# Attention scores as whole-array matmuls of stacked, rounded operands that GpSimd prepares, in a two-layer encoder

## The chip, the cores and the metric

The kernel runs on one core of one Trainium2 chip. A core has a matrix engine (TensorE, in the profile PE, and PEld for its loads of weights), VectorE (DVE), ScalarE (ACT), GpSimd (POOL) and a queue engine (SP) that issues transfers. The metric is the device time of one execution in microseconds.

## The reference, cut to what matters

Two layers on 256 tokens of 1024 numbers, in float32. Layer 0 mixes tokens by a gated convolution, layer 1 by attention in a window; behind each stands a retrieval of experts by product keys (PEER). The change touches the scores of the attention:

```
qkv = x @ w_qkv                       # 16 query heads, 4 key/value heads, 64 numbers each
scores = einsum("bnqhgd,bnkhd->bnhgqk", q, kw) / sqrt(HEAD_DIM)
logits = where(valid, scores + bias, NEG_INF)
probs  = softmax(concat([logits, sink_logit]))[..., :-1]
out    = einsum("bnhgqk,bnkhd->bnqhgd", probs, vw) @ w_o
```

With 256 tokens and a window of 128 a head has a score matrix of 256 x 256, cut to the window by its bias.

## The kernel before, in words

Nearly all products are made on TensorE in a rounded float32 form (F32R) that TensorE takes faster than full float32. To keep the precision each weight tile is split: ScalarE rounds it (`hi`, L189) and VectorE takes the remainder (`lo`, L190). The activations are kept as such pairs too, and a product is the sum of lo x hi, hi x hi and hi x lo. The weights stream through SP's queue in one fixed order; `take` hands out the next pair and starts the split of a later one.

The attention (`attention`) comes between the two PEER parts and lasts from about 874 to 960 us in the profile. It starts with the keys (`bk`), query block 0 and the values. A query block is 128 columns, two heads of 64, one on partitions 0 to 63 and one on 64 to 127, and there are eight blocks. `factors` and L455 scale the keys, L756 makes the factor of the queries, L758 scales query block 0 and L674 the others. Queries and keys lie in full float32 in `qk`. Key block n holds the two key heads that query blocks 4n to 4n + 3 use.

Then a loop of eleven steps: step s does `values(s-3)` (tile po), `scores(s)` (psc), `turned(s-2)` (transposes of the probabilities, ppt), `project(s-4)` (pwo), `queries(s+2)` (pq) and `softened(s)` (the softmax, on ScalarE and VectorE), as far as these exist. `in_turn` puts each behind TensorE's last instruction, so that TensorE runs them in this order; the other engines' instructions are placed by a scheduler that goes by readiness. `scores(c)` before: for each half of the tokens t and each of the two heads i a matmul of 64 partitions in full float32, which the profile shows as two instructions:

```
r = slice(HD * i, HD * i + HD)
matmul(b[i][:, t], qk[r, c, P * t : P * t + P], qk[r, kc], start=True, stop=True)
```

VectorE adds bias to the scores and takes the row minimum (L690) straight from PSUM.

GpSimd's queue holds only transfers here: in steps 0, 2, 4, 6 and 8 `blank_part` (L570) writes zeros over a part of the table that the second PEER part will fill. Each part waits for the transfer of the one before and for the last remainder that VectorE has made (`bg.behind`).

Of the kernel before, what the change touches and what calls it, by code (L numbers as in the profile page):

```python
# [8 lines left out]
F32 = mybir.dt.float32  # L9
F32R = mybir.dt.float32r  # L10
# [4 lines left out]
ALU = mybir.AluOpType  # L15
AX = mybir.AxisListType

P = 128
T = 256
D = 1024  # L20
NT = T // P
KC = D // P
HEADS = 16
HD = 64
# [52 lines left out]
def trunk_kernel(  # L77
# [21 lines left out]
    V, S, G, PE = nc.vector, nc.scalar, nc.gpsimd, nc.tensor  # L99

    const = ctx.enter_context(tc.tile_pool(name="const", bufs=1))
    big = ctx.enter_context(tc.tile_pool(name="big", bufs=1))
# [8 lines left out]
    def matmul(*a, **k):  # L111
        newest[:] = [PE.matmul(*a, **k).ins]  # L112
        return newest[0]
# [5 lines left out]
    def in_turn():  # L119

        return tc.issue_after(newest[0])
# [11 lines left out]
    def bank(tag, name):  # L133
        if tag == "acc":
            return four_banks(False).tile([P, 512], F32, tag=tag, name=name, bufs=4)
        return ps.tile([P, 512], F32, tag=tag, name=name, bufs=2)
# [77 lines left out]
    def take(n=2):  # L214

        prefetch(n)
        return ahead.popleft()
# [8 lines left out]
    def cols_product(dst, w, act, nth=None):  # L226

        hi, lo = (a.rearrange("p (k c) -> p k c", k=KC) for a in w)
        if nth == 0:
            turns = [(w, k, n) for w, n in ((hi, 0), (lo, 0), (hi, 1)) for k in range(KC)]  # L230
        elif nth == 1:
            turns = [(w, k, n) for w, n in ((hi, 0), (hi, 1), (lo, 0)) for k in range(KC)]
        else:
            turns = [(lo, k, 0) for k in range(KC)] + [(hi, k, n) for k in range(KC) for n in range(2)]
        for i, (w, k, n) in enumerate(turns):
            matmul(dst, w[:, k], act[:, k, T * n : T * n + T], start=(i == 0), stop=(i == 3 * KC - 1))
# [216 lines left out]
    def times_factor(dst, b, n):  # L453

        V.tensor_tensor(  # L455
            dst, b.rearrange("p (a t) -> p a t", a=n), yb[:, None, :].to_broadcast([P, n, T]), ALU.mult
        )
# [190 lines left out]

    def attention(sc, last):
        bias, sk = sc.held  # L650
        qk = sc(10, T)
        vt = sc(NT, T)
        both = big.tile([P, 2, KC, 2 * T], F32R, tag="HB", name="xo")
        bk = bank("u", "pk")
# [2 lines left out]

        ring = [(sc(2, 2, T + 1), sc(2, 2, 2, P), sc(2, 2, 2)) for i in range(3)]
        yq = sc(T)

        def all_values(i, bv):
            hi, lo = (a.rearrange("p (k c) -> p k c", k=4) for a in take())
            for t in range(NT):
                for k in range(4):
                    xh = xn[:, 4 * i + k, P * t : P * t + P]
                    xl = xn[:, 4 * i + k, T + P * t : T + P * t + P]
                    matmul(bv[t][:, :T], xh, lo[:, k], start=(i == 0 and k == 0), stop=False)
                    matmul(bv[t][:, :T], xh, hi[:, k], start=False, stop=False)
                    matmul(bv[t][:, :T], xl, hi[:, k], start=False, stop=(i == 1 and k == 3))

        def queries(c):
            b = bank("acc" if 4 <= c < 6 else "g", "pq")
            cols_product(b[:, :T], take(), xn)
            V.tensor_tensor(qk[:, c], b[:, :T], yq, ALU.mult)  # L674

        def scores(c):

            p, _, s = ring[c % 3]
            kc = KC + c // 4
            V.tensor_copy(p[:, :, :, T], sk[:, 2 * c : 2 * c + 2, None].to_broadcast([P, 2, NT]))  # L680
            b = [bank("u", "psc").rearrange("p (t k) -> p t k", t=2) for i in range(2)]
            for t in range(NT):
                for i in range(2):
                    r = slice(HD * i, HD * i + HD)
                    matmul(b[i][:, t], qk[r, c, P * t : P * t + P], qk[r, kc], start=True, stop=True)
            for t in range(NT):
                for i in range(2):
                    j0 = 383 - P * (1 - t)
                    h = 2 * c + i
                    V.tensor_tensor_reduce(  # L690
                        p[:, i, t, :T], b[i][:, t], bias[:, h, j0 : (j0 - T if j0 >= T else None) : -1],
                        1.0, sk[:, h : h + 1], ALU.add, ALU.min, s[:, 0, i, t : t + 1],
                    )
# [48 lines left out]
        def do(f, c, *a):  # L742
            with in_turn():
                f(c, *a)

        cols_product(bk[:, T:], take(), xn, 1)
        b0 = bank("u", "pq")
# [6 lines left out]
        with tc.issue_after(evicted[0]):  # L754
            copied[:] = [S.activation(stat[:, 10:11], eps, AF.Exp).ins]
        V.tensor_scalar(yq, yb, -1.0 / 8.0, None, op0=ALU.mult)  # L756
        times_factor(qk[:, KC:], bk, 2)
        V.tensor_tensor(qk[:, 0], b0[:, :T], yq, ALU.mult)  # L758
        with in_turn():
            all_values(1, pair)  # L760
        do(queries, 1)
        for t in range(NT):
            S.activation(vt[:, t], pair[t][:, :T], AF.Copy, scale=stat[:, 8 + t : 9 + t])

        for s in range(KC + 3):
            if s in (0, 2, 4, 6, 8):
                blank_part(nc.gpsimd, bg.behind)
            if s >= 3:
                do(values, s - 3)
            if s < KC:  # L770
                do(scores, s)
            if s == KC - 1:
                do(project, s - 4, lambda: do(turned, s - 2))
            else:
                if 2 <= s < KC + 2:
                    do(turned, s - 2)
                if 4 <= s < KC + 2:
                    do(project, s - 4)
            if s + 2 < KC:
                do(queries, s + 2)  # L780
            if s < KC:
                with tc.issue_after(copied[0]):
                    softened(s)
# [498 lines left out]
    sc = Scratch("HA", "mix0")  # L1282
# [11 lines left out]
    last = peer(0, last, prepare_attention)  # L1294
    blank_table()
    last = attention(held.pop(), last)

    def last_row(part):
# [49 lines left out]
    for n, (t, c) in enumerate(ends):  # L1348
        h = c.start // 512
        if c.start == 768:  # L1350
            b = bank("u", "pend")[:, :T]
# [99 lines left out]
```

## Time and profile before

| | us |
|---|---|
| median of 3 runs | 1740.62 (1739.82 to 1740.95) |
| profiled execution | 1739.6 |
| its span | 1737.8 |
| TensorE busy | 1729.0 |
| VectorE busy | 1383.1 |
| GpSimd busy | 995.4 |
| in the stretch 866 to 960: TensorE, VectorE, ScalarE, GpSimd busy, of 94.0 | 93.9, 68.9, 64.3, 5.8 |

A row of the profile names line, engine, operation, the tile written and the tile read. The chain goes back from the last instruction to whatever released each step. In the groups, busy time counts overlapping instructions once, while the mean duration of a matmul holds its way through the array as well. The granted clock of TensorE is 0.999 of full speed over the span.

### The profile page before, as it was taken

How to read it: one execution, taken by the hardware profiler on the slowest of the kernel's cores; microseconds unless marked ns; L12 is line 12 of the kernel's file. 1: busy time of each engine (PE TensorE's matmuls, PEld its weight loads, DVE VectorE, ACT ScalarE, POOL GpSimd, SP SyncE). 2: the span in 40 equal slices, each digit the busy share in tenths (PEclk: the TensorE clock that was granted, in tenths of full speed). 3: DMA queues.
4: the chain of work that ended last, by engine and by line, in shares of the span. 5: the costliest groups of instructions: out<-in, count | busy, mean ns of one | idle time of the engine just before them, and what ended most of it. 6: DMA issues, size and time to landing. Idle time of an engine off the chain costs nothing.

```text
span 1737.8 us, 28407 instructions
## 1 busy us (share of the span) xinstructions
PE 1729.0 (99%) x9801; PEld 1486.7 (86%) x9801; DVE 1383.1 (80%) x2996; ACT 946.9 (54%) x1274; POOL 995.4 (57%) x592
## 2 busy tenths in 40 slices
PE   9999999999999999999999999999999999999998
PEld 8989888888898888888898898888888888888886
DVE  8879999887877677777686899898887867777776
ACT  5455665565555444444476656655655544444444
POOL 1002888878888888500000048888788888881000
PEclk9999999999999999999999999999999999999999
DMA  7786998777769899998765779987776799997884
GB/s 246 245 285 212 277 280 197 169 190 171 183 182 237 226 238 242 286 286 260 228 207 169 255 212 284 256 196 171 190 176 164 202 240 230 236 246 251 259 261 148
DMA packets 292592, 390.80 MB, mean 225 GB/s; under 512 B 120181, under 2 KB 209813, under 8 KB 292192
## 3 DMA queue, kind: packets, MB, share of 16 engines
q1 hardware_dynamic: 86976, 314.35, 54.1%
q0 software_dynamic: 79904, 22.17, 14.4%
q10 hardware_dynamic: 125568, 52.48, 11.6%
q8 instruction: 76, 1.25, 0.3%
q14 instruction: 68, 0.56, 0.1%
HBM read 352.95 MB, written 35.95 MB: 224 GB/s over the span
## 4 chain that ended last, share of the span: by engine, by line
PE 98%; DVE 1%; DMA 1%; issue 0%; ACT 0%; SPq 0%; ACTq 0%
PE ph L112 41%; PE pv L112 40%; PE pq L112 6%; PE pconv L112 3%; PE pgate L112 1%; PE psc L112 1%; PE pwo L112 1%; PE pout L112 1%; PE pg L112 1%; PE ppt L116 0%; PE po L112 0%; PE pk L112 0%; DVE xs L335 0%; DMA gates<-table 0%; DMA xs<-in_x 0%; PE ptr L116 0%
## 5 line engine op out<-in xcount | busy, mean ns | idle before, releaser
L190 DVE TENSOR_TENSOR lo<-raw,hi 128x1024 fp32r<-128x1024 f32 (+1 forms) x597 | 722.5, 1220 | 227.4 <-ACT hi L189 163.3
L189 ACT CAST hi<-raw 128x1024 fp32r<-128x1024 f32 x595 | 623.7, 1050 | 489.1 <-PE pv L112 163.1
L582 POOL DMA_INDIRECT table<-route x256 | 448.5, 1752 | 130.0 <-issue 71.9
L112 PE MATMUL pv<-hi,xn 128*128 128x512 f32 (+1 forms) x2048 | 507.9, 389 | 0.0
L112 PE MATMUL ph<-xn,hi 128*128 128x512 f32 (+1 forms) x2112 | 491.4, 385 | 0.0
L112 PEld LDWEIGHTS pv<-hi,xn 128*128 128x128 f32 x2048 | 384.3, 188 | 79.7
L112 PEld LDWEIGHTS ph<-xn,hi 128*128 128x128 f32 x2112 | 380.3, 188 | 70.6
L582 POOL DMA_INDIRECT far_table<-yb x192 | 379.6, 1977 | 58.6 <-issue 51.0
L112 PE MATMUL pv<-lo,xn 128*128 128x512 f32 x1024 | 277.3, 390 | 0.3 <-DVE lo L190 0.2
L112 PEld LDWEIGHTS ph<-xn,lo 128*128 128x128 f32 x2048 | 262.0, 191 | 9.1
L112 PE MATMUL ph<-xn,lo 128*128 128x256 f32 x2048 | 269.2, 284 | 0.0
L112 PEld LDWEIGHTS pv<-lo,xn 128*128 128x128 f32 x1024 | 191.3, 188 | 40.3 <-ACT xn L1243 1.0
L1220 POOL DMA_DIRECT2D far_gates<-far_table x44 | 23.9, 543 | 231.0 <-DVE route L1237 115.4
L570 POOL DMA_DIRECT2D table<-blank x16 | 18.7, 1168 | 214.5 <-DVE lo L190 164.2
L582 POOL DMA_INDIRECT set_table<-yb x64 | 117.3, 1833 | 26.0 <-issue 18.6
L1243 ACT CAST xn<-hm 128x512 fp32r<-128x512 f32 x64 | 39.9, 623 | 76.8 <-PE pv L112 64.8
L1244 DVE TENSOR_TENSOR xn<-hm,xn 128x512 fp32r<-128x512 f32 x64 | 44.1, 690 | 37.6 <-ACT xn L1243 25.2
L295 ACT COPY hm<-ph 128x512 f32<-128x512 f32 x62 | 36.4, 587 | 58.7 <-PE ph L112 31.1
L112 PE MATMUL pq<-xr,hi 128*128 128x512 f32 (+1 forms) x288 | 65.7, 373 | 0.2
L1174 ACT ACTIVATE hm<-hm 128x512 f32<-128x512 f32 x62 | 39.1, 631 | 41.8 <-DVE hm L296 41.6
L112 PEld LDWEIGHTS pq<-xr,hi 128*128 128x128 f32 x288 | 50.4, 188 | 9.8 <-ACT xr L379 0.8
L295 ACT COPY route<-ph 128x512 f32<-128x512 f32 x62 | 36.1, 583 | 28.4 <-PE ph L112 23.6
(218 smaller groups left out, 1518.2 us busy)
## 6 DMA issues: line engine op xcount, KB each, us to landing
raw<-in_u SPq DMA_DIRECT2D x256, 512.0 KB
raw<-in_v SPq DMA_DIRECT2D x256, 512.0 KB
table<-blank POOLq DMA_DIRECT2D x16, 1024.0 KB
raw<-in_w_q SPq DMA_DIRECT2D x32, 512.0 KB
gates<-table ACTq DMA_DIRECT2D x128, 128.0 KB
raw<-in_w_in SPq DMA_DIRECT2D x23, 512.0 KB
far_table<-blank ACTq DMA_DIRECT2D x10, 1024.0 KB
far_gates<-far_table ACTq DMA_DIRECT2D x156, 64.0 KB
```

What stands on the lines that cost most here:

```text
L112: newest[:] = [PE.matmul(*a, **k).ins]
L189: bg.rounded = (G.tensor_copy if pieces > 1 else S.copy)(hi[:, c], raw[:, c]).ins
L190: bg.behind = V.tensor_tensor(lo[:, c], raw[:, c], hi[:, c].bitcast(F32), ALU.subtract).ins
L295: S.copy(dst, b[:, :, T:])
L570: ins = queue.dma_start(dst, blank[:, None, :].to_broadcast([P, dst.shape[1], P])).ins
L582: nc.gpsimd.indirect_dma_start(to, bass.IndirectOffsetOnAxis(ap=places[:, c : c + 1], axis=0), gates[:, c : c + 1], None, compute_op=ALU.a ...
L1174: S.activation(hm[:, j : j + 2], hm[:, j : j + 2], AF.Gelu)
L1220: ins = (nc.gpsimd if i == 2 else nc.scalar).dma_start(f[:, i], part.rearrange("p (a e t) -> p a e t", a=2, e=2)).ins
L1243: copied[:] = [S.copy(a[:, 0], src).ins]
L1244: return V.tensor_tensor(a[:, 1], src, a[:, 0].bitcast(F32), ALU.subtract).ins
```

## The change: what it does, and the diff

The scores are made of rounded operands. For each head a query block is laid out over all 128 partitions: its rounded half on the head's own 64 partitions, its remainder on the other 64 (`stacked_query`). The keys are laid out twice over the 128 partitions: once the rounded keys on both halves, once their remainders on both halves (`stacked_keys`). A matmul with the first sums rounded query x rounded key and remainder x rounded key, one with the second adds the two other products, in the same bank. A call of scores is now eight matmuls of 128 partitions where it was eight instructions of 64.

The copies that round and the subtractions that leave the remainder are new instructions of 64 partitions x 256 numbers. For a query block they are two roundings and two subtractions on GpSimd; block 0 has its subtractions on VectorE. For key block 0 ScalarE rounds the own halves, GpSimd the others, VectorE and GpSimd subtract; for key block 1 GpSimd does all eight. The stacks take the place of a tile of the PEER part before (`xa`), and the scaled queries go to a ring of two.

```
-        qk = sc(10, T)
+        kf, qf = sc(2, T), [sc(T) for _ in range(2)]
...
+        stacks = big.tile([P, KC, 2 * T], F32R, tag="xa", name="stacks").rearrange("p k c -> p (k c)")
+        keys = stacks[:, : 8 * T].rearrange("p (n i s c) -> p n i s c", n=2, i=2, s=2)
+        query = [stacks[:, 2 * T * (4 + i) : 2 * T * (5 + i)].rearrange("p (i c) -> p i c", i=2) for i in range(3)]
+        sides = slice(0, HD), slice(HD, P)
+
+        def stacked_keys(n, rounds, subtracts):
+            for i, (own, other) in enumerate((sides, sides[::-1])):
+                rounds(keys[own, n, i, 0], kf[own, n])
+                G.tensor_copy(keys[other, n, i, 0], kf[own, n])
+                for to, subtract in ((own, subtracts), (other, G.tensor_tensor)):
+                    subtract(keys[to, n, i, 1], kf[own, n], keys[own, n, i, 0].bitcast(F32), ALU.subtract)
+
+        def stacked_query(c, b, subtracts):
+            q, to = qf[c % 2], query[c % 3]
+            V.tensor_tensor(q, b, yq, ALU.mult)
+            for i, (own, other) in enumerate((sides, sides[::-1])):
+                G.tensor_copy(to[own, i], q[own])
+                subtracts(to[other, i], q[own], to[own, i].bitcast(F32), ALU.subtract)
...
-            V.tensor_tensor(qk[:, c], b[:, :T], yq, ALU.mult)
+            stacked_query(c, b[:, :T], G.tensor_tensor)
...
-                    r = slice(HD * i, HD * i + HD)
-                    matmul(b[i][:, t], qk[r, c, P * t : P * t + P], qk[r, kc], start=True, stop=True)
+                    for s in range(2):
+                        matmul(
+                            b[i][:, t], query[c % 3][:, i, P * t : P * t + P], keys[:, c // 4, i, s],
+                            start=(s == 0), stop=(s == 1),
+                        )
...
-        times_factor(qk[:, KC:], bk, 2)
-        V.tensor_tensor(qk[:, 0], b0[:, :T], yq, ALU.mult)
+        times_factor(kf, bk, 2)
+        stacked_query(0, b0[:, :T], V.tensor_tensor)
+        stacked_keys(0, S.copy, V.tensor_tensor)
         with in_turn():
             all_values(1, pair)
         do(queries, 1)
+        stacked_keys(1, G.tensor_copy, G.tensor_tensor)
```

GpSimd's order at the attention, before the change; the first row is the end of the PEER part, `route` with `in_subk` the start of the next one (mix is the scratch of the attention, set_table and far_table are tables of the PEER part):

```order
L582 DMA far_table_110<-yb 1048576x1 x32
L582 DMA far_table_111<-yb 1048576x1 x32
L1220 DMA far_gates<-far_table_111 128x128 x22
L570 DMA table<-blank 128x16x128 x5
L793 DMA route_9840<-in_subk 128x2048
```

The five blanks follow each other with nothing between. After the change, GpSimd's first rows behind far_gates; L667 and L668 are the roundings of the keys on their own and on the other partitions, L670 the keys' remainders, L676 and L677 rounding and remainder of a query block:

```order
L668 CAST stacks<-mix_7407 64x256 x2
L676 CAST stacks<-mix_7407 64x256 x2
L670 TENSOR_TENSOR stacks<-mix_7407,stacks 64x256 x2
L667 CAST stacks<-mix_7407 64x256
L668 CAST stacks<-mix_7407 64x256
L670 TENSOR_TENSOR stacks<-mix_7407,stacks 64x256 x2
L667 CAST stacks<-mix_7407 64x256
L668 CAST stacks<-mix_7407 64x256
L670 TENSOR_TENSOR stacks<-mix_7407,stacks 64x256 x2
L570 DMA table<-blank 128x16x128
L676 CAST stacks<-mix_7407 64x256 x2
L677 TENSOR_TENSOR stacks<-mix_7407,stacks 64x256 x2
```

The first three rows belong to key block 0 and query block 0, the six behind them to key block 1, then come the first blank and query block 1. Behind these stand query block 2, the second blank, query block 3, the third blank, query blocks 4, 5 and 6, the fourth blank, query block 7 and the fifth blank.

VectorE's order at the same place, with its waits, after the change (L455 scales the keys, the first L674 query block 0, the second query block 1; L190 are remainders of weights for the next query products):

```order
L455 TENSOR_TENSOR mix_7407<-pk,yb 128x512
L674 TENSOR_TENSOR mix_7407<-pq,mix_7407 128x256 [waits DVE_49]
L670 TENSOR_TENSOR stacks<-mix_7407,stacks 64x256 [waits Activation_49] x2
L677 TENSOR_TENSOR stacks<-mix_7407,stacks 64x256 [waits Pool_49] x2
L190 TENSOR_TENSOR lo<-raw,hi 128x1024 [waits DMAHW3_49,PE_49]
L190 TENSOR_TENSOR lo<-raw,hi 128x1024 [waits DMAHW4_49,PE_49,Activation_49]
L674 TENSOR_TENSOR mix_7407<-pq,mix_7407 128x256 [waits PE_49]
```

Before the change the rows L670 and L677 were not there and the first L674 was L758; now the four subtractions stand ahead of the two L190, and the second pair of them waits for GpSimd.

More of the change, by code (lines that the diff above doesn't have):

```diff
@@ L673, in queries @@
             cols_product(b[:, :T], take(), xn)
-            V.tensor_tensor(qk[:, c], b[:, :T], yq, ALU.mult)
+            stacked_query(c, b[:, :T], G.tensor_tensor)
         def scores(c):
-            p, _, s = ring[c % 3]
-            kc = KC + c // 4
+            p = ring[c % 3][0]
             V.tensor_copy(p[:, :, :, T], sk[:, 2 * c : 2 * c + 2, None].to_broadcast([P, 2, NT]))
@@ L683, in scores @@
                 for i in range(2):
-                    r = slice(HD * i, HD * i + HD)
-                    matmul(b[i][:, t], qk[r, c, P * t : P * t + P], qk[r, kc], start=True, stop=True)
+                    for s in range(2):
[3 more added lines that the diff above has]
+                        )
+            s = ring[c % 3][2]
             for t in range(NT):
```

## The prediction

> **What bounds the kernel now.** I read the page first: the span, the engines' shares and the chain that ended last.
>
> ```profile
> span 1737.8 us, 28407 instructions
> PE 1729.0 (99%) x9801; PEld 1486.7 (86%) x9801; DVE 1383.1 (80%) x2996; ACT 946.9 (54%) x1274; POOL 995.4 (57%) x592
> PE 98%; DVE 1%; DMA 1%; issue 0%; ACT 0%; SPq 0%; ACTq 0%
> ```
>
> TensorE is the chain almost alone, so a microsecond that TensorE gains or loses anywhere reaches the end nearly whole. The score matmuls are therefore priced on TensorE. In the groups by shape they are this row:
>
> ```profile
> L112 PE MATMUL psc<-mix 64*128 64x256 f32 x64 | 9.1, 402 | 0.0
> ```
>
> That is 64 instructions in eight calls of scores, eight to a call. A mean of 402 ns is a latency, since matmuls overlap; what a call costs is read from the chain in order of time, here from the last query product ahead of scores(0) to scores(4) (columns: start, length, work):
>
> ```profile
> 890.48 2.88 PE pq L112 x24
> 893.35 1.06 PE psc L112 x8
> 894.42 3.07 PE pq L112 x24
> 897.49 1.06 PE psc L112 x8
> 898.55 3.07 PE pq L112 x24
> 901.62 1.06 PE psc L112 x8
> 902.68 1.03 PE ppt L116 x8
> 903.71 2.87 PE pq L112 x24
> 906.58 1.02 PE po L112 x16
> 907.60 1.06 PE psc L112 x8
> 908.67 1.03 PE ppt L116 x8
> 909.69 2.87 PE pq L112 x24
> 912.57 1.02 PE po L112 x16
> 913.59 1.06 PE psc L112 x8
> ```
>
> The reader is to see three things: the pieces follow each other without a gap; a call of scores is 1.06 us; and a query product directly behind a call takes 3.07 us where one elsewhere takes 2.87 us, so each of the first two calls costs another 0.20 us.
>
> **Part 1, the matmuls (removed and added).** A query product is 24 whole-array matmuls of 128x256 in the rounded form, so one takes 2.87 / 24 = 0.12 us. The new scores are eight of the same shape and form: 8 x 0.12 = 0.96 us instead of 1.06, and I let the 0.20 us behind the first two go, since neighbours are then of one kind. Gain: 8 x 0.10 + 2 x 0.20 = 1.2 us. Bounds: 0.4 us if a switch of shape costs 0.1 us a call, 2.0 us if the second matmul of a pair, which keeps its weights, saved another 0.1 us a call. Nothing in this part can bring more than 2 us, 0.12%. A measurement of this kernel tells about 0.2% (3.5 us) from no change.
>
> **Part 2, GpSimd before scores(1).** GpSimd stood free here but for its transfers:
>
> ```profile
> 891.79 1.18 POOL L570 DMA_DIRECT2D table<-blank  x1 [50.34 <-DVE lo L190]
> 900.02 1.17 POOL L570 DMA_DIRECT2D table<-blank  x1 [7.05 <-DVE mix L690]
> 908.11 1.15 POOL L570 DMA_DIRECT2D table<-blank  x1 [6.92 <-DVE mix L707]
> ```
>
> Now it prepares operands that TensorE waits for, and the order of its queue, listed in the section on the change, decides when. Its first six instructions are what scores(0) needs (L668, L676, L670). Then come eight (two rounds of L667, L668 and L670) for the second pair of key heads, not needed before scores(4), then the table's first part (L570), and only then query 1 (L676, L677), which scores(1) needs. All of it starts when the keys are scaled (L455) on VectorE:
>
> ```profile
> 888.99 0.68 DVE L455 TENSOR_TENSOR mix<-pk,yb 128x512 f32<-128x512 f32 x1
> 889.59 0.41 DVE L758 TENSOR_TENSOR mix<-pq,mix 128x256 f32<-128x256 f32 x1
> 890.27 1.22 DVE L190 TENSOR_TENSOR lo<-raw,hi 128x1024 fp32r<-128x1024 f32 x1 [0.27 <-PE pv L112]
> 891.96 1.23 DVE L190 TENSOR_TENSOR lo<-raw,hi 128x1024 fp32r<-128x1024 f32 x1 [0.46 <-ACT hi L189]
> 896.07 1.22 DVE L190 TENSOR_TENSOR lo<-raw,hi 128x1024 fp32r<-128x1024 f32 x1
> ```
>
> The start is 888.99 + 0.68 = 889.67. The GpSimd rows that come nearest in price are a rounding of twice the length and an instruction of one element:
>
> ```profile
> L189 POOL CAST hi<-raw 128x512 fp32r<-128x512 f32 x2 | 1.2, 614 | 4.4 <-DMA raw<-in_w_in 4.4
> L157 POOL IOTA token<- 128x1 f32 x1 | 0.2, 152 | 0.0
> ```
>
> A rounding of 256 elements: 0.15 + (0.61 - 0.15) / 2 = 0.38 us. GpSimd's subtract is in no row. From below it is 0.38 us; from above two such passes, 0.76; I take 0.61, the rounding of 512, because it reads as many elements, 2 x 256. Up to the end of query 1: ten roundings, 3.8; eight subtracts, 4.9; one issue of the blank, 1.2; together 9.9 us, so 899.6. TensorE would be at scores(1) at 893.35 + 0.96 + 2.87 = 897.2 and through it at 898.1. Its third matmul needs the last of the four instructions of query 1, so six matmuls lie behind: 899.6 + 0.72 = 900.3, a stall of 2.2 us with GpSimd running freely.
>
> It will hardly run freely. At the start of the kernel GpSimd and VectorE met twice (the timeline, and the spread of durations of the remainders, least, median, greatest):
>
> ```profile
> 1.30 1.50 POOL L155 IOTA iota<- 128x256 bf16 x1
> 1.72 1.16 DVE L152 TENSOR_SCALAR ident<-ident 128x128 f32<-128x128 f32 x1
> 7.87 1.20 POOL L189 CAST hi<-raw 128x512 fp32r<-128x512 f32 x2 [4.38 <-DMA raw<-in_w_in]
> 8.52 1.70 DVE L190 TENSOR_TENSOR lo<-raw,hi 128x512 fp32r<-128x512 f32 x2 [0.37 <-POOL hi L189]
> L190 DVE TENSOR_TENSOR lo<-raw,hi x597: 680/1220/1277, 8.5 to 1723.5; 128x1024 fp32r<-128x1024 f32 x198, 128x512 fp32r<-128x512 f32 x1
> ```
>
> The comparison ended at 2.88, just behind the index fill's end at 2.80. Of the two half-length remainders one took the least, 0.68 us, so the other 1.70 - 0.68 = 1.02 us: it began at 8.52 inside GpSimd's rounding and finished 0.47 us behind its end at 9.07. Both read as one engine waiting out the other. So I add VectorE's instructions with two inputs in SBUF to the 9.9 us: four new subtracts at about 0.35 us (between 1.22 / 4 = 0.31 and L758's 0.41), 1.4; and two remainders of weights, 2.4; the third falls beside the blank. Query 1 is then done at 889.7 + 9.9 + 3.8 = 903.4, scores(1) at 904.1, a stall of 6.0 us. If the meeting only stretched an instruction by 1.02 - 0.68 = 0.34 us, six meetings would add 2.0 us instead of 3.8 and the sum below would be 1.8 us smaller.
>
> The Trainium skill, "SBUF — State Buffer", section "SBUF: two separate sides", calls the port pair that the two engines share an exclusive lock, held for a whole instruction, against VectorE instructions with two SBUF inputs among others; the two meetings agree, with 0.34 us or more of waiting in each. By it the third remainder would count too, 1.2 us more.
>
> **Part 3, VectorE.** It gets the four subtracts (L670, L677) behind its scaling of query 0, ahead of two weight remainders (L190) and of query 1's scaling (L674), as the second listing shows. The two L190 now stand behind a wait for GpSimd's roundings (L677), so the one for query product 2, done at 891.5 before, comes some 3 us later, about when TensorE asks for it near 894.5. Scores(0) and that product can lose up to 0.8 us together; this lies inside the wait for query 1, which is later by more, so I add nothing. The two extra roundings of ScalarE and the same scalings (L674 for L758) I cost at nothing: TensorE's value and query matmuls up to 893.35 cover them; uncovered they were 0.8 us, two of at most L758's 0.41.
>
> **Part 4, the blanks.** Each part of the table waits for the transfer of the one before: the starts 891.79, 900.02, 908.11 are 8.1 to 8.2 us apart. Query 4's preparation stands behind the third. With the first at B, query 1 ends at B + 3.2 and scores(1) at B + 3.9; TensorE's pieces up to scores(4) are 2.87 + 0.96 + 1.03 + 2.87 + 1.02 + 0.96 + 1.03 + 2.87 + 1.02 = 14.6 us, so it stands there at B + 18.5. The third blank starts at B + 16.3 and query 4 is ready at B + 16.3 + 1.2 + 2.0 = B + 19.5. Third matmul instead of B + 18.8: 0.7 us lost. Bounds: nothing if the transfers run faster, 2 us if weight remainders get between. Later queries have 8.7 us a step and no blank just ahead.
>
> **The sum.** -1.2 + 6.0 + 0.7 = +5.5 us. The profiled execution took 1739.6 us, of which 1737.8 are its span; this gives 1745.1. The median of the runs shown is 1740.62, 1.0 above it: **1746.1 us**. This is the forecast, its own range 1743.5 to 1748, chance 0.50.
>
> **The rivals.** *The engines overlap after all* (ends as no change): GpSimd runs freely, 9.9 us alone, stall 2.2: -1.2 + 2.2 + 0.7 = +1.7, 1742.3; with subtracts at 0.38 some 1.8 less, 1740.5. For it: only two meetings are seen, both at the start. Against it: both waited. It decides where query 1 is ready by 901.4 instead of 903.4 (a sum of 3.5 us). Chance 0.24.
>
> *The array slows down after the stall*: TensorE, which now is idle for 8.8 us in all (1737.8 - 1729.0), would start slowly again behind a long wait, as it does at the beginning:
>
> ```profile
> 1.08 2.74 PE L112 MATMUL pwarm<-blank 128*128 128x512 bf16 x6 [1.08 <-DVE blank L172]
> 4.52 0.85 PE L112 MATMUL pwarm<-blank 128*128 128x512 bf16 x2
> 7.81 1.03 PE L112 MATMUL pwarm<-blank 128*128 128x512 bf16 x4
> ```
>
> Six took 2.74 us, 0.46 each, later four 1.03, 0.26 each. If the slow stretch lasts from 1.08 to 4.52, 3.4 us at about half speed, it costs 1.7 us: 1747.8. For it: the stall of 6 us. Against it: other work may break the stall into pieces. Chance 0.18. The Trainium skill, "TensorE: Matmul & The Clock Gate", section "Part 1: The HAM clock gate", has the array fall to half rate after an idle window of about 3.4 us; no run here has yet shown an idle stretch of that length in mid-kernel.
>
> *Every step pays*: GpSimd's queue stays late in all steps, 1 us for each of scores(2) to (7): 1746.1 + 6 = 1752. Against it: from scores(5) on a step is 8.7 us and four instructions take 2. Chance 0.06.
>
> *Faster by over 0.2%* has no term here: at most 2.0 us can be gained. Chance 0.02 for what I have not seen.
>
> **How the numbers follow.** The range goes from the free rival, near its cheap end, 1741.0, to the forecast with the third remainder (1.2), subtracts at 0.76 (1.2) and the slow array (1.7), about 1750.0. Slower by over 0.2% is above 1744.1: 0.46 of the forecast's 0.50, 0.18 and 0.06, 0.70. Within 0.2%: 0.24 and 0.04, 0.28. Faster: 0.02.
>
> **What would show it.** In the changed kernel's chain: psc pieces of 0.96 us with pq at 2.87 behind them; a wait of TensorE for GpSimd at scores(1) of 4 to 7 us and one below 2 us at scores(4); subtracts on GpSimd near 0.6 us; roundings and subtracts longer beside L190, or L190 longer beside them; the first blank near 900. I am wrong if query 1 is ready by 898, if psc takes more than 1.06 us a call, or if the waits come at every step.

## The result and the profile after

| | before | after |
|---|---|---|
| median, us | 1740.4 (1739.82 to 1740.95, 6 runs) | 1749.93 (1747.94 to 1750.24, 6 runs) |
| span of the profiled execution, us | 1737.8 | 1748.0 |
| granted clock over the span | 0.999 | 0.998 |
| length of the attention, us | 69.44 | 78.69 |

The change makes the kernel slower: the ratio of the times is 1.0054, 95% interval 1.0044 to 1.0064, or 9.5 us. Here and below "length of the attention" runs from the first matmul of query product 1 (pq from xo, directly behind the values) to the first matmul of the PEER part behind (pq from xr): 890.31 to 959.75 before, 891.12 to 969.81 after. It grew by 9.25 us. Up to its start TensorE runs alike in all traces: query product 1 begins 15.96 to 15.98 us behind the first matmul of the keys (pk). That matmul itself lies anywhere from 873.99 to 875.28 us; so the 0.8 us by which the profiled attention starts later here is no part of the account.

The code of the attention has moved down: L690 is now L711 (minimum of the scores), L703, L705, L707 are L724, L726, L728, L699 is L720 and L733 is L754. First the page, the lines that answer to those of before: TensorE is no longer the whole chain.

```profile
span 1748.0 us, 28475 instructions
PE 1731.0 (99%) x9801; PEld 1490.9 (85%) x9801; DVE 1388.3 (79%) x3000; ACT 947.5 (54%) x1276; POOL 1016.0 (58%) x634
PE 96%; DVE 1%; POOL 1%; DMA 1%; issue 0%; ACT 0%; SPq 0%; DVEq 0%; ACTq 0%; POOLq 0%
```

The chain in order of time (start, length, work), from the end of GpSimd's work on key block 1 to scores(4):

```profile
902.36 1.16 POOL table L570
...
904.02 0.41 POOL stacks L676
904.43 0.07 issue
904.50 0.73 POOL stacks L677
905.23 0.04 issue
905.27 0.80 PE psc L112 x2
...
906.07 1.65 PE psc L112 x6
907.72 3.90 PE pq L112 x24
911.62 0.96 PE psc L112 x8
912.58 0.87 PE ppt L116 x8
...
924.26 1.15 PE psc L112 x8
925.42 0.87 PE ppt L116 x8
```

The blank (L570) and query 1 (L676, L677) are the last things that scores(1) waits for, as the order of the queue said. The matmuls behind them are slow for a while: six score matmuls take 1.65 us and the query product 3.90, where it took 2.87 before. TensorE's timeline names its waits (in brackets the idle time and who ended it):

```profile
894.00 0.52 PE L112 MATMUL psc<-stacks 128*128 128x256 f32 x3
895.66 0.86 PE L112 MATMUL psc<-stacks 128*128 128x256 f32 x5 [1.14 <-POOL stacks L670]
905.27 2.45 PE L112 MATMUL psc<-stacks 128*128 128x256 f32 x8 [5.88 <-POOL stacks L677]
...
919.72 0.66 PE L116 MATMUL ppt<-ident,mix 128*128 128x128 f32 x4 [0.78 <-DVE xo L754]
```

Three waits: 1.14 us inside scores(0), 5.88 us at scores(1), 0.78 us at a transpose. There is none at scores(4). The granted clock stands in the busy times by stretch (the column ahead of the DMA share, the last but two):

```profile
905.20:906.00 0.80, 0.73 (x2) 0.50 (x2) 0.00 (x0) 0.00 (x0) 0.72 (x2) 0.50 0.96 271
...
909.00:910.00 1.00, 1.00 (x6) 1.00 (x6) 0.54 (x3) 0.94 (x4) 0.91 (x1) 0.53 0.00 0
910.00:911.00 1.00, 1.00 (x11) 1.00 (x10) 0.74 (x1) 0.00 (x0) 0.28 (x1) 1.00 0.08 25
```

Behind the wait of 5.88 us the clock is 0.50 for about 4.7 us, from 905.27 to about 909.95. It had fallen during the wait, at 903.1, that is 3.7 us after TensorE fell idle (899.39); so it was low for 6.8 us in all. What GpSimd did meanwhile, in its timeline and in the durations of the tile stacks (least, median, greatest in ns):

```profile
890.64 0.99 POOL L668 CAST stacks<-mix 64x256 fp32r<-64x256 f32 x2 [48.59 <-DVE mix L455]
...
892.97 2.64 POOL L670 TENSOR_TENSOR stacks<-mix,stacks 64x256 fp32r<-64x256 f32 x2
895.67 1.28 POOL L667 CAST stacks<-mix 64x256 fp32r<-64x256 f32 x1
...
904.50 1.51 POOL L677 TENSOR_TENSOR stacks<-mix,stacks 64x256 fp32r<-64x256 f32 x2
```

```profile
L676 POOL CAST stacks<-mix x16: 386/398/657, 891.7 to 941.6; 64x256 fp32r<-64x256 f32 x16
L677 POOL TENSOR_TENSOR stacks<-mix,stacks x14: 717/728/737, 904.5 to 942.9; 64x256 fp32r<-64x256 f32 x14
L670 POOL TENSOR_TENSOR stacks<-mix,stacks x6: 718/738/1587, 893.0 to 901.6; 64x256 fp32r<-64x256 f32 x6
L667 POOL CAST stacks<-mix x2: 1282/1289/1296, 895.7 to 899.0; 64x256 fp32r<-64x256 f32 x2
```

A rounding takes 0.40 us and a subtract 0.73 when nothing meets them. Both roundings of L667 took 1.29, 0.89 more than L668's 0.40: each began while VectorE was at a remainder of weights. The two engines stretch each other: VectorE's two remainders there took 3.32 us for twice 1.22.

```profile
893.38 3.32 DVE L190 TENSOR_TENSOR lo<-raw,hi 128x1024 fp32r<-128x1024 f32 x2
898.57 1.52 DVE L190 TENSOR_TENSOR lo<-raw,hi 128x1024 fp32r<-128x1024 f32 x1
912.78 1.26 DVE L726 TENSOR_SCALAR mix<-mix 128x257 f32<-128x257 f32 x2
913.96 0.89 DVE L728 TENSOR_SCALAR mix<-mix 128x257 f32<-128x257 f32 x1
```

### The profile page after: what moved, and what is told of

Its sections match the earlier page's. It is cut to its first block, busy times and chain, and to the rows that moved or that the text cites. A ratio compares the mean times of both kernels' runs of the same rounds, so it can differ in the third digit from the quotient of the medians.

```text
span 1748.0 us, 28475 instructions
## 1 busy us (share of the span) xinstructions
PE 1731.0 (99%) x9801; PEld 1490.9 (85%) x9801; DVE 1388.3 (79%) x3000; ACT 947.5 (54%) x1276; POOL 1016.0 (58%) x634
## 3 DMA queue, kind: packets, MB, share of 16 engines
q8 instruction: 77, 1.26, 0.3%
## 4 chain that ended last, share of the span: by engine, by line
PE 96%; DVE 1%; POOL 1%; DMA 1%; issue 0%; ACT 0%; SPq 0%; DVEq 0%; ACTq 0%; POOLq 0%
PE ph L112 41%; PE pv L112 40%; PE pq L112 6%; PE pconv L112 2%; PE psc L112 1%; PE pwo L112 1%; PE pout L112 1%; PE pg L112 1%; PE pgate L112 1%; PE po L112 0%; PE ppt L116 0%; DMA raw<-in_w_in 0%; DMA xs<-in_x 0%; PE pk L112 0%; POOL stacks L670 0%
## 5 line engine op out<-in xcount | busy, mean ns | idle before, releaser
L190 DVE TENSOR_TENSOR lo<-raw,hi 128x1024 fp32r<-128x1024 f32 (+1 forms) x597 | 723.6, 1222 | 229.8 <-ACT hi L189 162.4
L582 POOL DMA_INDIRECT far_table<-yb x192 | 374.6, 1951 | 58.6 <-issue 51.6
L570 POOL DMA_DIRECT2D table<-blank x16 | 19.0, 1186 | 134.2 <-DVE lo L190 106.7
```

Source lines behind the costliest of these rows:

```text
L190: bg.behind = V.tensor_tensor(lo[:, c], raw[:, c], hi[:, c].bitcast(F32), ALU.subtract).ins
L570: ins = queue.dma_start(dst, blank[:, None, :].to_broadcast([P, dst.shape[1], P])).ins
L582: nc.gpsimd.indirect_dma_start(to, bass.IndirectOffsetOnAxis(ap=places[:, c : c + 1], axis=0), gates[:, c : c + 1], None, compute_op=ALU.a ...
```

## The experiments

The theory: the loss is made at the start of the attention by the order of GpSimd's queue (TensorE waits for query 1 behind key block 1 and a blank), with the slow clock behind that wait as its second part; the matmuls themselves gain. The rivals: the whole-array matmuls are not faster; or the work of rounding, done anywhere, disturbs the other engines, and this is the loss. All kernels were timed beside the kernel before (its median 1740.1 us for the first eight of them, 1740.2 for the last two). Diffs are against the changed kernel. In the diffs S is ScalarE, V VectorE and G GpSimd.

**e1_matmuls_alone**: the new matmuls on a tile filled once; no rounding, no subtracting. It leaves out the preparation, so its scores are not the reference's.

```
+        for i in range(4):
+            G.tensor_copy(stacks[:, 896 * i : 896 * i + 896], xs[:, 0, :896])
...
-            for i, (own, other) in enumerate((sides, sides[::-1])):
-                G.tensor_copy(to[own, i], q[own])
-                subtracts(to[other, i], q[own], to[own, i].bitcast(F32), ALU.subtract)
...
-        stacked_keys(0, S.copy, V.tensor_tensor)
...
-        stacked_keys(1, G.tensor_copy, G.tensor_tensor)
```

> The new matmuls alone: the stacks are filled once, early in the attention, from other data, and the preparation of keys and queries is left out, so the scores are not those of the reference. Theory (TensorE waits for GpSimd's preparation, the matmuls themselves are a little cheaper): 1739.5 us, 0.9 below the kernel before (1740.4), no wait at scores(0) or scores(1). Rival (the whole-array matmuls are the dearer ones, by weights or by switching shape): 1742 or more without any wait.

Measured 1738.46 us, ratio 0.9992 [0.9983, 1.0001]; the attention is 68.00 us long, 1.44 shorter than before. Its chain of waits is TensorE alone:

```profile
894.29 0.96 PE psc L112 x8
895.25 2.88 PE pq L112 x24
898.13 0.96 PE psc L112 x8
...
907.70 1.16 PE psc L112 x8
908.86 0.87 PE ppt L116 x8
```

A call is 0.96 us behind a query product, with 2.88 for the product that follows. Behind the values (po) it is 1.15, but the transposes behind it then take 0.87: together 2.02 or 2.03 where before it was 1.06 + 1.03 = 2.09. So the matmuls do gain, by 1.44 us in this trace; in the time alone so little can hardly be told from nothing, and the interval holds 1.

**e2_preparation_alone**: the reverse. All roundings and subtractions are made, but the scores are the old matmuls of full float32 and read none of it.

```
-                    for s in range(2):
-                        matmul(
-                            b[i][:, t], query[c % 3][:, i, P * t : P * t + P], keys[:, c // 4, i, s],
-                            start=(s == 0), stop=(s == 1),
-                        )
+                    r = slice(HD * i, HD * i + HD)
+                    matmul(b[i][:, t], qk[r, c, P * t : P * t + P], qk[r, KC + c // 4], start=True, stop=True)
```

> The preparation alone: GpSimd, ScalarE and VectorE make all stacks as in the change, but the scores are made by the old matmuls from float32 operands and nobody reads the stacks. Theory (the loss is TensorE's wait for query 1 and what follows from it): 1740 to 1742 us, since VectorE's remainders have some slack. Rival (the loss is VectorE held up by GpSimd at the shared access to memory, which delays remainders and softmax for TensorE): 1745 or more, most of the 9.5 us, with TensorE waiting for VectorE.

Measured 1741.94 us, ratio 1.0009 [1.0000, 1.0018]; 1.9 us above the kernel before; the attention of the profiled execution is 71.84, 2.40 longer, but its keys' factor began 0.6 us later against TensorE than before, behind a transfer of weights. This is what the preparation costs by being in the way of other engines when no matmul waits for it. The chain shows it at VectorE: behind subtractions that wait for GpSimd stands the weight remainder that query product 2 needs.

```profile
893.59 1.65 DVE lo L190
...
895.37 3.10 PE pq L112 x24
```

So about 2 us of the 9.3 can be disturbance that reaches TensorE in this way; the rest needs that TensorE waits for the operands. That wait holds disturbance of its own, since GpSimd's instructions are stretched too.

**e4_kept_warm**: the change, with twenty throw-away matmuls ahead of scores(1), so that TensorE works through the wait.

```
+            if s == 1:
+                with in_turn():
+                    keep_warm(20)
```

> The changed kernel with 20 extra matmuls of zeros on TensorE ahead of scores(1), inside its wait. Theory (the wait of 6 us lets the clock fall to one half, and that costs 1.7 us behind it): 1748.2 us, 1.7 below the change (1749.9), granted clock 1.00 from 905 to 911, the wait unchanged. Rival (the low clock in the records costs nothing): 1749.9 or a little more.

Measured 1746.66 us, ratio 1.0040 [1.0026, 1.0053]; attention 76.01, 2.68 shorter than with the change, and more than was expected. GpSimd's work and the time at which query 1 is ready stay the same. Now scores(1) comes after the throw-away work, still behind GpSimd, and the clock stays at 1.00 in every stretch (busy times, the column ahead of the DMA share):

```profile
898.91 4.49 PE L112 MATMUL pwarm<-blank 128*128 128x512 bf16 x20
904.94 0.50 PE L112 MATMUL psc<-stacks 128*128 128x256 f32 x2 [1.54 <-POOL stacks L677]
```

```profile
905.20:909.20 4.00, 3.70 (x31) 3.50 (x31) 2.68 (x9) 2.08 (x8) 3.58 (x6) 1.00 0.57 166
```

The query product behind is back at 2.88 us. Counted from the start of the attention, TensorE is 1.7 us earlier at its end than with the change; the other 1.0 us is the wait at the transpose at 919.72, which has no counterpart here. The slow clock is thus shown to cost 1.7 us at its place. That the 1.0 us at the transpose follows from it is not shown; the two came and went together in this pair.

**e10_order_alone and e6_reordered**: only the order of GpSimd's queue is changed. Key block 1 goes behind query 3 (it is first needed by scores(4)), and the blanks come in steps 2, 4, 6, 8 and 9. e6 has, besides, ScalarE round query block 0 (the first line), e10 has not.

```
+                (G.tensor_copy if c else S.copy)(to[own, i], q[own])
...
-        stacked_keys(1, G.tensor_copy, G.tensor_tensor)
...
-            if s in (0, 2, 4, 6, 8):
+            if s in (2, 4, 6, 8, 9):
...
+            if s == 1:
+                with tc.issue_after(made[0]):
+                    stacked_keys(1, G.tensor_copy, G.tensor_tensor)
```

> The change with another order on GpSimd: ScalarE rounds query 0, query 1 comes directly behind key block 0, key block 1 behind query 3, the blanks start in step 2 instead of 0. All the same work is done. Theory (it is the place in the queue, not the amount): stalls at scores(0) and scores(1) together under 1.5 us, no fall of the clock, 1739.5 to 1742 us. Rival (the amount of work on GpSimd, or its meetings with VectorE in each step): 1744 or more.

> The reordered kernel, but with query 0 rounded by GpSimd as in the change: only the order of GpSimd's queue differs from the change (key block 1 behind query 3, first blank two steps later). If the order of the queue is the cause: scores(1) waits 1 to 2 us where it waited 6, the clock stays at 1.00, 1743 to 1744.5. If it were the two roundings of query 0 on GpSimd that made the queue late: 1747 or more.

Measured: e6 1742.67 us, ratio 1.0013 [1.0004, 1.0022], attention 72.06; e10 1743.16, ratio 1.0016 [1.0007, 1.0025], attention 72.56. The time of e6 lies between what was expected and its rival, that of e10 at the place expected of it. The order alone (of key block 1 and the blanks together) takes 6.1 of the 9.25 us away (78.69 - 72.56). In e10's timeline of TensorE the wait at scores(1) is 0.84 instead of 5.88, and the clock is 1.00 throughout:

```profile
895.43 0.86 PE L112 MATMUL psc<-stacks 128*128 128x256 f32 x5 [1.14 <-POOL stacks L670]
...
900.25 0.98 PE L112 MATMUL psc<-stacks 128*128 128x256 f32 x6 [0.84 <-POOL stacks L677]
...
904.87 0.98 PE L112 MATMUL psc<-stacks 128*128 128x256 f32 x6 [0.53 <-POOL stacks L677]
...
913.26 0.66 PE L116 MATMUL ppt<-ident,mix 128*128 128x128 f32 x4 [1.05 <-DVE xo L754]
```

**e3_keys_late**: key block 1 behind query 2, the blanks where the change has them. The scheduler then put the second blank ahead of query 2 and key block 1 ahead of query 3.

```
-        stacked_keys(1, G.tensor_copy, G.tensor_tensor)
...
+            if s == 0:
+                with tc.issue_after(made[0]):
+                    stacked_keys(1, G.tensor_copy, G.tensor_tensor)
```

> The change with key block 1 prepared behind query 2 instead of ahead of query 1; the scheduler then puts the second blank, which waits some 8 us for the transfer of the first, ahead of query 2. Theory (what stands ahead of a query in GpSimd's queue is what TensorE waits for): the wait at scores(1) shrinks from 6 us to 1 or 2, and a new one of 2 to 4 us appears at scores(2), behind the second blank; 1743 to 1745 us. Rival (eight instructions less ahead of query 1 are all there is to it): 1742 or less, no wait at scores(2).

Measured 1748.62 us, ratio 1.0047 [1.0033, 1.0060], attention 78.67: nothing gained, where the order in e10 gains 6.1, and later than was expected. The timeline shows that the wait moved one call on:

```profile
899.30 0.98 PE L112 MATMUL psc<-stacks 128*128 128x256 f32 x6 [0.85 <-POOL stacks L677]
907.70 2.44 PE L112 MATMUL psc<-stacks 128*128 128x256 f32 x8 [4.54 <-POOL stacks L677]
916.49 0.50 PE L112 MATMUL psc<-stacks 128*128 128x256 f32 x2 [1.00 <-POOL stacks L677]
```

```profile
897.66 1.60 POOL stacks L677
...
904.42 0.27 DVE mix L728
...
904.76 1.19 POOL table L570
```

In e3's chain (the last fence) GpSimd was through with query 1 at 899.26, and its next instruction in the queue, the blank, began at 904.76; query 2 stood behind it. Of the things that a blank waits for, the trace speaks for VectorE: its L728 was done at 904.69, while the last packet of the blank before had moved by 903.1. So it was not the transfer, as I had expected; no run tests this further. Behind the 4.54 us the clock fell as in the change, to 0.60 on average from 907.70 to 912.00. So the wait belongs to whatever stands in the queue ahead of the next query, not to scores(1).

**e5_without_gpsimd, e7_rounded_by_scalar, e8_one_step_earlier**: the work goes to other engines. In e5 ScalarE rounds everything and VectorE subtracts everything, with key block 1 behind query 3 (the expectation says query 2). e7 is e6 with all query blocks rounded by ScalarE. e8 is e7 with every query product one step earlier, its weights with it.

```
-                G.tensor_copy(to[own, i], q[own])
+                S.copy(to[own, i], q[own])
...
-            stacked_query(c, b[:, :T], G.tensor_tensor)
+            stacked_query(c, b[:, :T], V.tensor_tensor)
...
+        do(queries, 2)
...
-            if s + 2 < KC:
-                do(queries, s + 2)
+            if s + 3 < KC:
+                do(queries, s + 3)
```

(The first change is in all three, the second in e5 alone, the rest in e8 alone.)

> The change with all rounding on ScalarE and all subtractions on VectorE, key block 1 behind query 2, the blanks as in the change. Theory (GpSimd's queue and its meetings with VectorE are the loss; VectorE itself has some room): 1740 to 1742 us; VectorE gets 0.84 us a step and is full in steps 0 to 2, so 1 to 2 us are lost there, no fall of the clock. Rival (the work is too much wherever it is done before scores(1)): 1744 or more.

> The reordered kernel (key block 1 behind query 3, blanks from step 2) with the queries' roundings on ScalarE, only their subtractions on GpSimd. Theory (each query waits in turn for GpSimd, whose instructions wait for VectorE's): GpSimd's part of a query falls from 2.3 to 1.5 us, the remaining waits at scores(1) and scores(2), 1 to 2 us each in the reordered kernel, halve; 1740 to 1742 us. Rival (VectorE, not GpSimd, is late): as the reordered kernel, 1742.7.

> As the run before, and each query product one step earlier, so that TensorE has another product of 2.9 us between a query and its scores. The order of the weights follows; all work is done. Theory (the matmuls are cheaper by 1.6 us, and with a step more of time nothing of the preparation is waited for): 1738.5 to 1740 us, as the matmuls alone. Rival (GpSimd's work costs VectorE so much in every step that TensorE waits for remainders or the softmax anyway): 1741 or more.

Measured 1745.71 us (ratio 1.0033 [1.0021, 1.0045], attention 75.65), 1743.20 (1.0019 [1.0010, 1.0028], 73.03) and 1743.63 (1.0020 [1.0011, 1.0029], 72.93). None reaches the time expected of it, and none beats e6. I had thought that ScalarE, 54% busy over the span, had room; here it had not. In e8 no call of scores waits any more, but the transposes of the probabilities wait for ScalarE's copy of the ones before (L737), which stands behind the roundings:

```profile
895.00 1.19 PE L112 MATMUL pq<-xo,lo 128*128 128x256 f32 x8 [0.92 <-DVE lo L190]
...
914.77 0.66 PE L116 MATMUL ppt<-ident,mix 128*128 128x128 f32 x4 [1.59 <-ACT mix L737]
...
921.59 0.66 PE L116 MATMUL ppt<-ident,mix 128*128 128x128 f32 x4 [0.68 <-ACT mix L737]
```

**e9_earlier_on_gpsimd**: e6 (roundings of queries 1 to 7 on GpSimd) with the query products one step earlier, as in e8.

> The reordered kernel with its query products one step earlier (query 2 in front of the loop, query s+3 in step s), roundings of queries 1 to 7 on GpSimd as there. Reordered it stood 2.6 us above the kernel before; about 1 us of that was TensorE waiting at scores(1) and 2 us at scores(2). If those waits are all that is left, they go: 1739.5 to 1740.5. If what is left is VectorE and ScalarE being late for the transposes (as in the version with ScalarE's roundings one step earlier, 1743.6), 1742 to 1744 and no wait in front of any scores.

Measured 1740.8 us, ratio 1.0004 [0.9995, 1.0013]: level with the kernel before, and the best version that computes the scores. The attention is 70.63 us, 1.2 more than before and 2.6 more than e1's. The waits for query operands are gone, as the first case had it, but what is left is of the second kind, if smaller than its 1742 to 1744:

```profile
894.29 1.19 PE L112 MATMUL pq<-xo,lo 128*128 128x256 f32 x8 [0.92 <-DVE lo L190]
...
913.23 0.66 PE L116 MATMUL ppt<-ident,mix 128*128 128x128 f32 x4 [0.83 <-DVE xo L754]
```

No version was found that beats both kernels; with e1 as the bound there are about 1.5 us, 0.1%, to be had.

## Why the prediction was right, and where its sizes were off

The sign, the place and the chief mechanism came out: slower, at scores(1), by GpSimd's queue. The forecast was 1746.1, with 1743.5 to 1748 as its own range, and the median is 1749.93: outside that, and inside the whole range by less than 0.1 us at its top. That it fell inside is in part luck, since terms that were missing or too small were set off in part by one that did not come. The rise is 9.5 us for the 5.5 of the sum. The places at which TensorE stands in the changed kernel, e4 and e1, each counted from the first matmul of its query product 1 (891.12, 890.79 and 891.25), give an account of the 9.25 us:

| term | forecast | measured, us | how worked out |
|---|---|---|---|
| matmuls | -1.2 | -1.4 | e1 against before: 68.00 - 69.44 |
| wait up to the end of scores(1) | +6.0 | +8.1 | e4 ends it 15.93 behind its start, e1 7.84 |
| slow clock behind it | a rival, +1.7 | +1.7 | to the end of the query product: 20.50 in the change, 18.80 in e4 |
| wait at a transpose | none | +1.0 | behind e1 by 9.78 at the end of scores(2), by 10.78 at the end of the second transposes (ppt) |
| blank ahead of query 4 | +0.7 | 0 | no wait at scores(4) |

The sum is -1.4 + 8.1 + 1.7 + 1.0 = 9.4, against 9.25 measured. The 5.88 us in the timeline is not the counterpart of the 6.0: it is one of the waits that make up the 8.1.

**Part 1** was right in kind and a little low: 0.96 us a call and 2.88 behind the first two, as priced, and another 0.06 to 0.07 a call where transposes follow. The upper bound, 2.0, held.

**Part 2** is the term that was mis-sized. Query 1 was to be ready 13.7 us after the keys are scaled; it was ready at 906.01, 15.5 after 890.48 (889.80 + 0.68, the end of L455). Of this, ten roundings at 0.40 are 4.0 (forecast 3.8); eight subtracts at 0.73 are 5.8 (4.9); the blank 1.16 (1.2); the 0.04 to 0.08 us that the chain calls issue between nearly any two GpSimd instructions, and the start, are about 1.1 (never counted); and the waits beside VectorE are 3.4 (3.8). So the waits of the two engines for each other were, in sum, nearly as large as I had taken them from two meetings at the kernel's start, and the miss is the subtract's price and the steps between instructions. The agreement of the waits is in part luck: 0.9 of the 3.4 is the meeting with the third remainder, which the sum had left out, so those that it counted cost 2.5 for 3.8. I had taken the subtract at 0.61 with 0.76 as its upper bound; the trace has 0.73. Another 0.3 us is the end of scores(1): its last six matmuls take 0.98 with the clock at full speed, where I had 0.72.

The Trainium skill, "GPSIMD Engine Reference", section "4.1 Engine selection", holds an elementwise operation of two inputs on GpSimd for about twice as slow as on VectorE. The runs show 0.73 against VectorE's 0.42 for the same subtract, 1.7 times; from the 0.35 that I had for VectorE the page would have given 0.70 as an estimate, nearer than my 0.61.

The third weight remainder, left out of the sum, also met GpSimd: the rounding of L667 at 899.05 took 1.30. The Trainium skill, "SBUF — State Buffer", section "SBUF: two separate sides", said so by its exclusive lock; what it cost here is 0.9 us, not the 1.2 that I worked out from it, as the remainder (898.57) was 0.5 us under way when the rounding began. The rival in which the engines overlap freely is out.

**The slow array** was put up as a rival against the forecast, with 0.18. It is no alternative: it needs the wait that the forecast has and comes on top of it. Its price, 1.7 us, came out to the tenth, in part by luck: its working (3.4 us at half speed) did not hold, since the clock stayed at 0.50 for 4.7 us of TensorE's work, in part of which it still waited for the second subtract. Forecast and rival together, 1747.8, would have been the better single number. The Trainium skill, "TensorE: Matmul & The Clock Gate", section "Part 1: The HAM clock gate", has the half rate too, and a window of about 3.4 us that runs freely, so that it need not begin with the work; the trace agrees, with a clock that was low for 6.8 us, two such windows, of which TensorE's work met 4.7.

**Part 3** put nothing on VectorE, and said that a loss at scores(0) of up to 0.8 us would lie inside the wait for query 1. It was 1.4 us (5.40 against e1's 4.00 at the end of scores(0)), and it did lie inside. What the step left out was VectorE's later work: L726 and L728, which read one tensor in SBUF and so were not in my list of instructions that meet GpSimd, took 1.26 for two and 0.89, where before they took about 0.62 and 0.35 (the same pair in e5, with GpSimd out of the way, takes 0.62). That this stretch is what made the transposes at 919.72 late is likely from the chain, which goes through VectorE there, but only their vanishing in e4 was shown.

**Part 4** was wrong in that the third blank delayed no query: the lateness of TensorE by then gave the queue its time, and the blanks themselves followed faster than the 8.1 to 8.2 us assumed (the second began 6.8 us after the first, released by its transfer). The third blank (917.56 to 918.74) met VectorE instead: the L726 of 917.99 beside it took 0.84 us, and it stands in the chain to the late transposes. e3 shows that the mechanism exists: there a blank ahead of query 2 sat in front of a wait of 4.54 us. **Every step pays** is out: from scores(4) on no query was late, in any run with GpSimd's roundings.

## What to carry to other kernels

When an idle engine is given work that another waits for, read its queue's order before its load: here GpSimd had nothing else to do in this stretch than blanks, and yet it was late; putting work that is needed four calls later, and the first blank, behind what is needed next took back two thirds of the loss. Price the queue as the sum of all that stands ahead of the item waited for, with the steps between instructions, and with the other engine's instructions that it meets. Both waits of TensorE of over 4.5 us here cost the idle time and then a second time at half clock, so a forecast of such a wait should hold both.

## What the runs showed of the hardware that was not expected

- An elementwise instruction on VectorE with one tensor in SBUF (128 x 257 float32) takes up to 0.89 us beside GpSimd's 64 x 256 subtracts, where alone it takes 0.35. Beside a blank it is stretched too, and was already before the change: there the L707 of 927.85 took 1.02 us beside the blank of 927.63. VectorE's instructions that read PSUM (L711) stay at 0.47 to 0.49.
- The clock fell to 0.50 at waits of 5.88 us and 4.54 (e3), not at 1.59 (e8, 1.00 throughout), but it did in e5 at a wait of 1.98 us; so the length of one wait does not give the rule. It was low for 3.4 us in e3 (907.8 to 911.2) and in e5 (914.0 to 917.4), and for twice that, 6.8, in the change (903.1 to 909.95). In the 3.4 us ahead of the fall TensorE was busy for 0.1 us in e3, 1.4 in e5 and 0 in the change. That reads as a clock set anew every 3.4 us by how busy TensorE was in the stretch before; three falls do not prove it.
- The same eight score matmuls are 0.96 us behind a query product and 1.15 behind the values' product, and transposes behind them 0.87 instead of 1.03: what a piece of TensorE costs depends on its neighbours by up to 0.2 us.
- Twenty matmuls of 128 x 512 that nobody reads, put into a wait, kept the clock up and were worth 1.7 us right behind it; the attention as a whole was 2.7 us shorter.
